# Three opening loads on another issuing queue, and a moved filter layer, in the prologue of a hybrid long-convolution and attention step

## The chip, the cores and the metric

The kernel runs on one core of a Trainium2 chip. The metric is the device time of one execution in microseconds (us). A program of one core is timed in several executions, and the median is given; one further execution is recorded by the hardware profiler.

## The reference, cut to what matters here

```python
shift, scale, gate = modulation(cond, w_ada, b_ada)        # silu(cond) @ w_ada + b_ada
h = x * (1 + scale) + shift                                # 128 context and 512 latent tokens, 1024 channels
hy, g_h, qkv, g_a, m = split(h @ w_in)                     # 10 x 1024 columns
z = concat([t, cos(bands * w), -sin(bands * w)])           # 33 features of each filter position
hf = sin(f_freq[0] * (z @ f_w1 + f_b1))                    # filter network, layer 1, 64 wide
hf = sin(f_freq[1] * (hf @ f_w2 + f_b2))                   # layer 2
y_h = long_conv(v_h, x1, x0, (hf @ f_w3) * decay)          # FFT convolution
y_a = attention(q, k, v)                                   # neighbourhood and context attention
out = (sigmoid(m) gates of (y_h*silu(g_h)) @ w_bh and (y_a*silu(g_a)) @ w_ba) @ w_out
x_new = layer_norm(ALPHA * x + gate * out)
```

All of it is in 32-bit floating point. The kernel gets this accuracy from TensorE's faster 32-bit form by cutting each operand into a high and a low part and adding three products (high by high, high by low, low by high).

## The kernel before, in words

All 640 tokens are held as columns; the 1024 channels lie in eight groups of 128 partitions. After an opening, the kernel works through 104 weight tiles of 128 output columns. A projection tile is 8 groups x 3 part products x 2 halves of 320 token columns: 48 products. The order on TensorE (PE), VectorE (DVE) and ScalarE (ACT) is written by hand in the opening; behind it a scheduler sets it, with a model of the time of each instruction. Every engine takes its own instructions in order.

**The opening** is `prologue` (from L267), a loop over the eight channel groups k. In each round

- SyncE (SP) issues two halves of modulation weights, `ada` (512 KB each, L258), and `xw` (L319, 512 KB: the group's tokens and three weight blocks). `xw` has three buffers (tag "raw", L307), which the later weight loads share; `ada` has three as well.
- PE multiplies the two halves by the conditioning vector (`adaT`, L262, 8 small products for each half). ACT copies the result (`row`, L318), PE turns it (`modT`, L341), DVE adds the biases (`mod`, L346).
- DVE and ACT make the modulated tokens: `hx` (L353) on DVE, the high part `hH` (L354) on ACT, the low part `hL` (L357) on DVE. `wf` (L328) and `wg` (L356) are the high and low parts of the three weight blocks.
- PE then makes the products of group k for tiles 0, 8 and 1 (`accumulate`, L172, its products stand at L177) in the next round; the table `script` (L268) says where. An entry "w3" in that table is three products of a zeroed operand (L281) whose result is thrown away; they fill PE's time.

Beside this runs **the filter network** (`hidden_layers`, L244). Each of its two layers (`sin_layer`, L222) is two products (L228), then a chain on DVE (L230 to L239) that reduces the angle, then ACT's sine (L241). The table `layers` (L272) says how many steps of it each round takes. Layer 1 works on `zemb` (33 x 640) and on `pack1` (128 x 196: both layers' weights, biases and frequencies); layer 2 on layer 1's `hf` and on `pack1`. The conditioning vectors and `sel` come in `pack0` (128 x 34). The buffer of `pack1` is used again for the first cached key block, `ck` (L865), so that load has to wait for the last reader of `pack1`, the two L230 of layer 2.

In the opening SP issues its loads in the order of the code: `pack0`, `zemb`, `pack1`, then round 0's `ada`. A load's completion is counted on one of eight counters in turn, and a load that would use a counter again waits for the load that used it before; so SP's order and the number of loads decide some of its waits.

**After the opening** come tiles 9 and 2, whose weights were loaded and split early, and then tile 10, the first whose low part is made by a transfer: ACT writes the negated high part to `wl` (L156) and GpSimd (POOL) issues a load of the weights that adds onto it (L157). Between them ACT and DVE evacuate the finished tiles 0, 8 and 1 (`zs`, L548 to L552), convolve them (`u` and `x`, L554 and L556), and split the transform's constants: `dftH` from `draw` (L381) and `gsH` from a block of `E` that the load `E<-gs` fills (L389, split at L391). The first filter products `fl` (L442, L443) need `w3h` and `w3l`, the split of the filter's last weights.

Of the kernel before, what the change touches and what calls it, by code (L numbers as in the profile page):

```python
# [46 lines left out]
def tile_hyena_natten_step(ctx: ExitStack, tc: tile.TileContext, a, o):  # L47
    nc = tc.nc
    P = 128

    def f(ap):
        return ap.bitcast(F32)
# [7 lines left out]
    pinned = [True]  # L60
    last = []

    def load_to(dst, src):
        ins = nc.sync.dma_start(dst, src)
        last[:] = [ins]
        if pinned[0]:
            tc.keep_in_program_order(ins)
# [33 lines left out]
    def aux(name):  # L101
        return ps_ax.tile([P, 512], F32, tag="aux", name=name)
# [9 lines left out]
    def row(pool, tag, name, dt=F32, bufs=NK + 1):  # L112
        return pool.tile([P, NT], dt, tag=tag, bufs=bufs, name=name)

    out = {"yh": {}}
    dram = ctx.enter_context(tc.tile_pool(name="dram", bufs=1, space=bass.MemoryType.DRAM))
    yh_d, ya_d, mh_d, ma_d = (dram.tile([NK, P, NT], F32, tag=t, name=t) for t in ("yh_d", "ya_d", "mh_d", "ma_d"))

    def load_pack(i):
        pack = const.tile([P, sum(n for _, n in PACKS[i])], F32, tag=f"pack{i}", name=f"pack{i}")  # L120
        load_to(pack[:], a[f"pack{i}"])
        c0 = 0
        for name, n in PACKS[i]:
            out[name] = pack[:, c0 : c0 + n]
            c0 += n

    v_d = dram.tile([4, P, 1280], F32, tag="v_d", name="v_d")

    load_pack(0)
    cc, sel = out["cc"], out["sel"]  # L130
    bss = const.tile([P, 2, NK], F32, tag="bss", name="bss")

# [7 lines left out]
    def wraw(i):  # L140
        raws[i] = wp.tile([P, 1024], F32, tag="raw", bufs=3, name=f"raw{i}")
        load_to(raws[i][:], a["wall"][i])
# [26 lines left out]
    def bank(i, ps_pair=None):  # L169
        return ps_pair or [acc(f"mm{i}_{hf}") for hf in range(2)]  # L170

    def accumulate(ps, w, k, xh, xl, lead=(0, 1, 2)):  # L172
        passes = (w[0], xh), (w[0], xl), (w[1], xh)
        for i in lead:
            wt, x = passes[i]
            for hf in range(2):
                nc.tensor.matmul(  # L177
                    ps[hf][:, :HALF], wt[k], x[:, hf * HALF : (hf + 1) * HALF],
                    start=(i == 0 and k == 0), stop=(i == lead[2] and k == NK - 1), skip_group_check=True,
                )  # L180
# [31 lines left out]
    def temp(tag, name, bufs=1):  # L212
        return hw.tile([P, NT], F32, tag=tag, bufs=bufs, name=name)
# [43 lines left out]
    def ada(ch, ps, raw):  # L257
        load_to(raw, a["wada"][ch])  # L258
        for t in range(2):
            for j in range(4):  # L260
                kt = 4 * t + j
                nc.tensor.matmul(  # L262
                    ps[32 * j : 32 * j + 32, :], st[:, kt, :], raw[:, P * kt : P * kt + P],
                    start=(t == 0), stop=(t == 1), skip_group_check=True, tile_position=(0, 32 * j),
                )

    def prologue():  # L267
        script = (  # L268
            ("w3", "w1", "w3", "w4"), ("", "", "00", "80 10"), ("", "", "01", "81 11"), ("", "", "02", "82 12"),
            ("", "", "03", "83 13"), ("", "", "04", "84 14"), ("", "", "05", "85 15"), ("", "", "06", "86 16 07 87 17"),  # L270
        )
        layers = ((1, 1), (0, 2), (0, 2), (0, 2), (1, 1), (0, 0), (0, 0), (0, 0))  # L272
        nc.vector.memset(f(hid[:, :256]), 0.0)
        front = (0, 8, 1)
        parts = {}

        def work(items):
            for item in items.split():
                if item[0] == "w":
                    for _ in range(int(item[1:])):  # L280
                        nc.tensor.matmul(banks[0][0][:, :256], hid[:, :P], hid[:, :256], start=True, stop=True, skip_group_check=True)  # L281
                else:
                    i, j = int(item[0]), int(item[1])
                    c = P * front.index(i)
                    accumulate(banks[i], [{j: t[:, c : c + P]} for t in parts[j]], j, hH[:, j], hL[:, j], lead=(0, 2, 1))

        def step(n):
            for _ in range(n):
                next(filt, None)

        out["zemb"] = temp("u", "zemb", 4)[:33]
        load_to(out["zemb"], a["zemb"])
        load_pack(1)
        th0 = const.tile([P, 2 * NK], F32, tag="th0", name="th0")
        spare = const.tile([P, 1], F32, tag="spare", name="spare")
        nc.gpsimd.memset(spare[:], 0.0)
        nc.scalar.activation(th0[:], cc, AF.Tanh, scale=0.5)
        nc.scalar.activation(spare[:], spare[:], AF.Sin)
        nc.vector.scalar_tensor_tensor(th0[:], th0[:], 1.0, cc, op0=ALU.add, op1=ALU.mult)
        nc.vector.tensor_scalar_mul(st[:, :, 0:2], th0[:].rearrange("p (k c) -> p k c", c=2), 0.5)  # L300
        nc.vector.tensor_copy(bss[:, 0], out["bss"][:, :NK])
        nc.vector.tensor_scalar_add(bss[:, 1], out["bss"][:, NK:], 1.0)
        for i in front:
            banks[i] = bank(i, (aux("mm1lo"), aux("mm1hi")) if i == 1 else None)
        filt = hidden_layers()
        for k in range(NK):
            xw = wp.tile([P, 1024], F32, tag="raw", bufs=3, name=f"xw{k}")  # L307
            psa = aux(f"adaT{k}")
            if k == 0:
                work("w12")  # L310
                step(7)
            pool, tag = ((hw, "X"), (hyc, "dftL"), (hw, "F"))[k % 3]
            wt = pool.tile([P, 2048], F32, tag=tag, name=f"ada{k}")
            for part in range(2):
                work(script[k][part])
                ada(part * 8 + k, psa[:, part * P : part * P + P], wt[:, 1024 * part : 1024 * part + 1024])
            row_ = hwa.tile([P, 2 * P], F32, tag="fb", bufs=3, name=f"row{k}")
            nc.scalar.activation(row_[:], psa[:, : 2 * P], AF.Copy)  # L318
            load_to(xw[:], a["xw"][k])  # L319
            xt, wf = xw[:, :NT], xw[:, NT:]  # L320
            wh = row(yhp, "yh", f"wf{k}", F32R)[:, : 3 * P]
            wl = row(yhp, "yh", f"wg{k}", F32R)[:, : 3 * P]
            parts[k] = wh, wl
            step(layers[k][0])
            if k >= 6:
                split(wh, wl, wf)
            else:
                nc.scalar.activation(wh, wf, AF.Copy)  # L328
            if k == 7:
                wraw(9)  # L330
                load_pack(2)
                out["convw"] = out["convw"].rearrange("p (i c) -> p i c", c=4)
                wraw(2)
                load_filter(0)
                out["dft"] = hw.tile([P, 2560], F32, tag="F", name="draw")
                load_to(out["dft"][:, :1280], a["dft"][:, :1280])
                w9 = hw.tile([P, 2, 1024], F32R, tag="X", name="w9")
            psm = aux(f"modT{k}")
            work(script[k][2])
            for c in range(2):  # L340
                nc.tensor.matmul(  # L341
                    psm[:, c * 2 : c * 2 + 2], row_[:, c * P : c * P + P], sel,
                    start=True, stop=True, skip_group_check=True,
                )
            mod = const.tile([P, 2, 2], F32, tag="mod", bufs=4, name=f"mod{k}")
            nc.vector.tensor_tensor(  # L346
                mod[:], psm[:, 0:4].rearrange("p (s c) -> p s c", s=2),
                bss[:, :, k : k + 1].to_broadcast([P, 2, 2]), op=ALU.add,
            )
            hx = hwa.tile([P, NT], F32, tag="cv", bufs=2, name=f"hx{k}")  # L350
            for c, s0, n in ((0, PC, LP), (1, SC, LS)):
                cs = slice(s0, s0 + n)
                nc.vector.tensor_scalar(hx[:, cs], xt[:, cs], mod[:, 1, c : c + 1], mod[:, 0, c : c + 1], op0=ALU.mult, op1=ALU.add)  # L353
                nc.scalar.activation(hH[:, k, cs], xt[:, cs], AF.Identity, scale=mod[:, 1, c : c + 1], bias=mod[:, 0, c : c + 1])  # L354
            if k < 6:
                nc.vector.tensor_tensor(wl, wf, f(wh), op=ALU.subtract)  # L356
            nc.vector.tensor_tensor(hL[:, k], hx[:], f(hH[:, k]), op=ALU.subtract)  # L357
            if k == 7:
                raw = raws.pop(9)
                nc.scalar.activation(w9[:, 0], raw[:], AF.Copy)  # L360
                low = nc.vector.tensor_tensor(w9[:, 1], raw[:], f(w9[:, 0]), op=ALU.subtract)
                early[2] = wtile(2)
                early[9] = [[w9[:, i, c : c + P] for c in range(0, 1024, P)] for i in range(2)]
            work(script[k][3])
            step(layers[k][1])
        now(filt)
        last.append(low)
# [1343 lines left out]
```

## Time and the profile before

| | us |
|---|---|
| three timed executions | 861.53, 862.32, 863.46 |
| their median | 862.32 |
| the profiled execution, its own time | 860.83 |
| its span, first to last instruction | 859.1 |
| PE busy in the span | 849.4 (99%) |
| DVE busy | 678.7 (79%) |
| ACT busy | 464.7 (54%) |

The span is 1.73 us shorter than the same execution's own time; what lies around the span is not in the profile. A PE that is shown as busy is not PE at its peak, since matmul ends are modelled; but where products follow one another at an even spacing, nothing but fewer or earlier products shortens the stretch. The page's mean transfer rate is 161 GB/s, and its first two slices of 21 us show 352 and 359.

### The profile page before, as it was taken

To read this page: it belongs to the slowest core of one execution; us is meant where nothing else is said; L and a number is where in the kernel's file an instruction comes from. 1 tells how busy PE (TensorE), PEld (TensorE's weight loads), DVE (VectorE), ACT (ScalarE), POOL (GpSimd) and SP (SyncE) were. 2 spreads that over 40 slices of the span, in tenths; PEclk is the share of its full clock that TensorE was granted. 3 is DMA by queue.
4 is the path that set the end of the run, shared out by engine and by line. 5 is a ranking of instruction groups with operands and counts; after the bars stand their busy time and mean duration, and the time that the engine had idled before them with its cause. 6 is when DMAs were issued, how large, how long until landed. Compare 5 with 4: busy or idle time off the path is not lost.

```text
span 859.1 us, 16817 instructions
## 1 busy us (share of the span) xinstructions
PE 849.4 (99%) x6387; PEld 822.7 (96%) x6387; DVE 678.7 (79%) x1408; ACT 464.7 (54%) x996; POOL 131.4 (15%) x140
## 2 busy tenths in 40 slices
PE   9999999999999999999999999999999999999996
PEld 7999999999999999999999999999999999999885
DVE  6777695697759559789988897889888778799776
ACT  4675656545554643646665676666655654345310
POOL 0010010101001010105232225124222200000000
PEclk9999999999999999999999999999999999999999
DMA  9986575656657558774263535354354386445621
GB/s 352 359 256 144 109 149 126 153 122 144 127 134 150 126 146 187 168 251 148 85 195 90 192 95 189 106 177 149 105 173 118 111 266 202 173 131 140 246 107 54
DMA packets 56868, 138.64 MB, mean 161 GB/s; under 512 B 8495, under 2 KB 23859, under 8 KB 56788
## 3 DMA queue, kind: packets, MB, share of 16 engines
q1 hardware_dynamic: 45412, 111.69, 39.7%
q0 software_dynamic: 5760, 20.19, 14.4%
q10 hardware_dynamic: 5616, 5.70, 1.9%
q8 instruction: 50, 0.82, 0.4%
q14 instruction: 30, 0.25, 0.1%
HBM read 121.43 MB, written 16.12 MB: 160 GB/s over the span
## 4 chain that ended last, share of the span: by engine, by line
PE 95%; DMA 3%; DVE 1%; SPq 0%; ACT 0%; issue 0%; DVEq 0%
PE sp L1182 33%; PE mm L177 30%; PE out L1534 6%; PE v L917 5%; PE pt L1019 3%; PE s L1026 3%; PE s L979 2%; PE mm L191 2%; PE ve L929 1%; DMA raw<-wall 1%; DMA wl<-wall 1%; DMA ada<-wada 1%; PE adaT L262 1%; PE yb L166 1%; PE yb L165 1%; PE yb L167 1%
## 5 line engine op out<-in xcount | busy, mean ns | idle before, releaser
L1182 PE MATMUL sp<-t,wb 128*128 128x320 f32 x912 | 141.7, 310 | 0.0
L1182 PEld LDWEIGHTS sp<-t,wb 128*128 128x128 f32 x912 | 134.9, 188 | 0.9 <-ACT pp L1047 0.5
L1182 PE MATMUL sp<-hH,wb 128*128 128x320 f32 x456 | 111.2, 314 | 0.0
L177 PE MATMUL mm<-hH,wl 128*128 128x320 f32 x448 | 105.5, 309 | 0.1
L177 PE MATMUL mm<-hH,wh 128*128 128x320 f32 x448 | 104.9, 309 | 0.0
L177 PE MATMUL mm<-hL,wh 128*128 128x320 f32 x448 | 104.2, 310 | 0.0
L157 POOL DMA_DIRECT2D wl<-wall x37 | 32.2, 870 | 329.5 <-ACT wl L156 263.3
L108 ACT ACTIVATE wb<-s 128x512 fp32r<-128x512 f32 x92 | 56.3, 627 | 45.6 <-DVE s L1142 26.6
L1182 PEld LDWEIGHTS sp<-hH,wb 128*128 128x128 f32 x456 | 78.4, 188 | 2.3 <-issue 2.1
L158 ACT ACTIVATE wh<-raw 128x1024 fp32r<-128x1024 f32 x37 | 39.2, 1059 | 70.8 <-PE mm L177 65.3
L177 PEld LDWEIGHTS mm<-hH,wl 128*128 128x128 f32 x448 | 75.5, 188 | 0.9 <-DMA wl<-wall 0.4
L177 PEld LDWEIGHTS mm<-hH,wh 128*128 128x128 f32 x448 | 75.2, 188 | 0.5
L177 PEld LDWEIGHTS mm<-hL,wh 128*128 128x128 f32 x448 | 75.1, 188 | 0.3
L109 DVE TENSOR_TENSOR wb<-s,wb 128x512 fp32r<-128x512 f32 x92 | 62.5, 692 | 10.3 <-ACT wb L108 10.3
L1182 PE MATMUL sp<-hL,wb 128*128 128x320 f32 x228 | 70.4, 309 | 0.0
L108 ACT ACTIVATE wb<-raw 128x512 fp32r<-128x512 f32 x66 | 41.4, 628 | 44.4 <-PE sp L1182 23.5
L1001 POOL TENSOR_SCALAR p<-p,sm 128x384 f32<-128x384 f32 x32 | 44.5, 1399 | 102.7 <-DVE sm L1000 102.7
L109 DVE TENSOR_TENSOR wb<-raw,wb 128x512 fp32r<-128x512 f32 x66 | 46.6, 705 | 5.5 <-ACT wb L108 5.4
L177 PE MATMUL mm<-yhs,wh 128*128 128x320 f32 x256 | 47.9, 309 | 0.0
L1197 DVE TENSOR_TENSOR c<-sp,u 128x320 f32<-128x320 f32 x69 | 33.5, 486 | 12.0 <-PE sp L1182 12.0
L1182 PEld LDWEIGHTS sp<-hL,wb 128*128 128x128 f32 x228 | 42.8, 188 | 0.0
L1001 POOL TENSOR_SCALAR edge<-edge,sm 128x320 f32<-128x320 f32 x32 | 41.9, 1318 | 0.5 <-DVE sm L1000 0.5
(385 smaller groups left out, 2078.3 us busy)
## 6 DMA issues: line engine op xcount, KB each, us to landing
raw<-wall SPq DMA_DIRECT2D x93, 512.0 KB, 3.6
wl<-wall POOLq DMA_DIRECT2D x37, 512.0 KB, 5.8
ada<-wada SPq DMA_DIRECT2D x16, 512.0 KB, 9.2
tm<-bias SPq DMA_DIRECT2D x16, 512.0 KB, 4.5
xw<-xw SPq DMA_DIRECT2D x8, 512.0 KB, 9.4
gate<-wgate SPq DMA_DIRECT2D x8, 512.0 KB, 4.1
wo<-wall SPq DMA_DIRECT2D x8, 512.0 KB, 5.3
dec<-decay SPq DMA_DIRECT2D x20, 128.0 KB, 3.0
```

The costliest lines, as they stand in the source:

```text
L108: hi = nc.scalar.activation(dst_h, src, AF.Copy)
L109: return hi, (eng or nc.vector).tensor_tensor(dst_l, src, f(dst_h), op=ALU.subtract)
L157: nc.gpsimd.dma_start(wl, a["wall"][i], accum_op=ALU.add)
L158: nc.scalar.activation(wh, raw[:], AF.Copy)
L177: nc.tensor.matmul(ps[hf][:, :HALF], wt[k], x[:, hf * HALF : (hf + 1) * HALF], start=(i == 0 and k == 0), stop=(i == lead[2] and k == NK - ...
L917: nc.tensor.matmul(ps[t // 2][:, t % 2 * 256 : t % 2 * 256 + 256], x[:, k, P * t : P * t + P], wk, start=first and t % 2 == 0, stop=last, ...
L1001: nc.gpsimd.tensor_scalar_mul(pv, pv, sm[:, 2:3])
L1019: nc.tensor.transpose(pt[:, i * P : i * P + P], x, ident)
L1026: nc.tensor.matmul(dst, lhs, rhs, start=start, stop=stop, skip_group_check=True)
L1182: nc.tensor.matmul(dst, wk, x(xi, k), start=j < 4 and k == 0 and i == 0, stop=k == 3 and i == 2, skip_group_check=True,)
L1197: after = nc.vector.tensor_tensor(c, dst, c if j == 3 else u, op=ALU.add)
L1534: ins = nc.tensor.matmul(dst, m[k][:, c0 : c0 + P], w[:, c : c + n], start=(first and k == 0), stop=(last and k == 5), skip_group_check=True,)
```

## The change

Three things change, all in the opening.

1. `pack0`, `zemb` and `pack1` are issued by ACT instead of SP, so SP's first load is round 0's `ada`.
2. The two products of the filter network's layer 2 move from behind round 0 to the middle of round 1: between the products of the two `ada` halves.
3. The filler products of round 0 go from 12, 3, 1, 3, 4 to 12, 2, 1, 3, 2.

```diff
-    def load_to(dst, src):
-        ins = nc.sync.dma_start(dst, src)
+    def load_to(dst, src, eng=nc.sync):
+        ins = eng.dma_start(dst, src)
...
-    def load_pack(i):
+    def load_pack(i, eng=nc.sync):
...
-        load_to(pack[:], a[f"pack{i}"])
+        load_to(pack[:], a[f"pack{i}"], eng)
...
-    load_pack(0)
+    load_pack(0, nc.scalar)
...
-            ("w3", "w1", "w3", "w4"), ("", "", "00", "80 10"), ("", "", "01", "81 11"), ("", "", "02", "82 12"),
+            ("w2", "w1", "w3", "w2"), ("", "", "00", "80 10"), ("", "", "01", "81 11"), ("", "", "02", "82 12"),
...
-        layers = ((1, 1), (0, 2), (0, 2), (0, 2), (1, 1), (0, 0), (0, 0), (0, 0))
+        layers = ((1, 0), (0, 2), (0, 2), (0, 2), (1, 1), (0, 0), (0, 0), (0, 0))
...
-        load_to(out["zemb"], a["zemb"])
-        load_pack(1)
+        load_to(out["zemb"], a["zemb"], nc.scalar)
+        load_pack(1, nc.scalar)
...
             for part in range(2):
                 work(script[k][part])
+                if k == 1 and part == 1:
+                    step(1)
                 ada(part * 8 + k, psa[:, part * P : part * P + P], wt[:, 1024 * part : 1024 * part + 1024])
```

Lines behind the insertion stand two lower in the changed kernel (L548 becomes L550). What the change moves on the engines, where it matters below:

On PE, from the transposed modulation of round 0 on (`modT0`; `ps_f640` are the products of layer 2, `adaT1` those of round 1's `ada` halves), the rows before were

```order
L341 MATMUL modT0_195<-pack0_84,row0_188 128x2 x2
L281 MATMUL mm0_0_134<-hid_93 128x256 x4
L228 MATMUL ps_f6400_214<-hf1_154,pack1_123 128x320
L228 MATMUL ps_f6401_215<-hf1_154,pack1_123 128x320
L262 MATMUL adaT1_221<-ada1_222,st_89 32x128 x16
L177 MATMUL mm0_0_134<-hH_87,wf0_191 128x320
```

and they are now

```order
L343 MATMUL modT0_194<-pack0_84,row0_187 128x2 x2
L281 MATMUL mm0_0_134<-hid_93 128x256 x2
L262 MATMUL adaT1_212<-ada1_213,st_89 32x128 x8
L228 MATMUL ps_f6400_223<-hf1_154,pack1_123 128x320
L228 MATMUL ps_f6401_224<-hf1_154,pack1_123 128x320
L262 MATMUL adaT1_212<-ada1_213,st_89 32x128 x8
L177 MATMUL mm0_0_134<-hH_87,wf0_190 128x320
```

The layer's two products stand eight small products later, and two fillers are gone here (one more stood behind layer 1). DVE's order in the opening is the same as before.

On ACT, behind the opening, the scheduler has set another order. Before, from the end of the evacuation of tile 0 on (`zs0`; `zs1` is tile 8, `u0` its first convolution):

```order
L552 ACTIVATE zs0_106<-mm0_1_135 128x8x40
L548 ACTIVATE zs1_110<-mm8_0_136 128x128
L550 ACTIVATE zs1_110<-mm8_0_136 128x8x8
L551 ACTIVATE zs1_110<-mm8_0_136 128x8x16
L552 ACTIVATE zs1_110<-mm8_1_137 128x8x40
L554 ACTIVATE u0_667<-zs0_106,pack2_601 128x641
L108 ACTIVATE w3h_0_694<-w3s0_696 128x512
```

and now

```order
L554 ACTIVATE zs0_106<-mm0_1_135 128x8x40
L108 ACTIVATE gsH_104<-E_100 128x256
L550 ACTIVATE zs1_110<-mm8_0_136 128x128
L552 ACTIVATE zs1_110<-mm8_0_136 128x8x8
L553 ACTIVATE zs1_110<-mm8_0_136 128x8x16
L554 ACTIVATE zs1_110<-mm8_1_137 128x8x40
L556 ACTIVATE u0_664<-zs0_106,pack2_598 128x641
L383 ACTIVATE dftH_102<-draw_608 128x640 x2
L108 ACTIVATE w3h_0_691<-w3s0_693 128x512
```

`gsH`, which stood behind `dftH` eleven rows further on, has moved ahead of the evacuation of tile 8; `dftH` has moved ahead of `w3h`. Behind these rows come, in both, the evacuation of tile 1 and the convolution `x`; then before `u1`, `wl10`, `wh10`, `wl3`, and now `wl10`, `wh10`, `u1`, `wl3` (`wl10` and `wh10` are tile 10's weights). On PE the first filter product moves 11 products later, and on DVE `gsL` and `dftL` come earlier. Behind tile 10 the orders are the same.

On SP the three small loads are gone from the front, and one load changes place. Before:

```order
L64 DMA ada3_340<-wada 128x1024 x2
L64 DMA xw3_338<-xw 128x1024
L64 DMA ada4_399<-wada 128x1024 x2
L64 DMA ck0_4395<-ck 128x128
L64 DMA xw4_397<-xw 128x1024
```

and now:

```order
L64 DMA ada3_337<-wada 128x1024 x2
L64 DMA xw3_335<-xw 128x1024
L64 DMA ck0_4392<-ck 128x128
L64 DMA ada4_396<-wada 128x1024 x2
L64 DMA xw4_394<-xw 128x1024
```

The load of `ck` stands ahead of round 4's `ada` now, so those wait on SP until `pack1`'s last reader is done.

## Prediction

> **What bounds the kernel now.** I read the page first, then busy time by stretch, then the chain that ended last at its beginning, then the engines' timelines there.
>
> ```profile
> PE 849.4 (99%) x6387; PEld 822.7 (96%) x6387; DVE 678.7 (79%) x1408; ACT 464.7 (54%) x996; POOL 131.4 (15%) x140
> ```
> ```profile
> 0.00:12.00 12.00, 10.14 (x101) 7.14 (x102) 6.70 (x19) 5.59 (x10) 0.87 (x16) 1.00 0.81 303
> 12.00:42.00 30.00, 30.00 (x355) 27.41 (x354) 21.44 (x44) 17.02 (x32) 0.00 (x0) 1.00 0.97 376
> 42.00:62.00 20.00, 19.91 (x135) 19.48 (x134) 15.87 (x24) 16.50 (x38) 2.74 (x3) 1.00 0.88 271
> 62.00:100.00 38.00, 38.00 (x270) 37.75 (x269) 25.57 (x45) 22.15 (x45) 3.45 (x4) 1.00 0.62 136
> ```
> ```profile
> 3.92 7.09 DMA ada<-wada
> 11.05 0.65 PE adaT L262 x16
> 11.69 1.07 PE mm L177 x6
> ...
> 49.73 1.07 ACT wl L156
> 51.11 7.61 DMA wl<-wall
> 58.77 1.15 PE mm L177 x6
> ```
>
> The first number behind a stretch is its length, the next PE's busy time. From 12 us on PE is full; only a fragment is missing at 42 to 62, where the chain shows PE waiting for the transfer that finishes tile 10's low weights. So the end moves by as much as PE's dense stretch starts earlier or later near 12 us, plus what PE loses around 58. The chain names what started it: the second half of round 1's `ada`, landed at 11.01. It is only the last of several things, as the timelines of PE, DVE and ACT (each asked alone) show:
>
> ```profile
> 1.17 2.93 PE L281 MATMUL mm<-hid 128*128 128x256 f32 x12 [1.17 <-DVE hid L273]
> 4.03 1.18 PE L228 MATMUL ps_f<-zemb,pack 33*64 33x320 f32 x4
> 11.62 0.56 PE L177 MATMUL mm<-hH,wf 128*128 128x320 f32 x2
> 12.31 0.46 PE L177 MATMUL mm<-hL,wf 128*128 128x320 f32 x2
> ```
> ```profile
> 5.26 0.61 DVE L230 TENSOR_SCALAR E<-ps_f,pack 128x320 f32<-128x320 f32 x1 [1.86 <-PE ps_f L228]
> 8.21 0.33 DVE L239 TENSOR_SCALAR E<-E 128x320 f32<-128x320 f32 x1
> 9.06 0.16 DVE L346 TENSOR_TENSOR mod<-modT,bss 128x4 f32<-128x4 f32 x1 [0.53 <-PE modT L341]
> 10.57 0.83 DVE L357 TENSOR_TENSOR hL<-hx,hH 128x640 fp32r<-128x640 f32 x1
> 11.32 1.12 DVE L230 TENSOR_SCALAR E<-ps_f,pack 128x320 f32<-128x320 f32 x2
> 13.14 0.16 DVE L346 TENSOR_TENSOR mod<-modT,bss 128x4 f32<-128x4 f32 x1 [0.70 <-PE modT L341]
> ```
> ```profile
> 8.57 0.47 ACT L241 ACTIVATE hf<-E 128x320 f32<-128x320 f32 x1 [0.20 <-DVE E L239]
> 9.36 1.19 ACT L354 ACTIVATE hH<-xw,mod 128x128 fp32r<-128x128 f32 x2
> ```
>
> There is a second chain, without slack inside. Layer 1's products (L228 at 4.03) feed DVE's angle chain, which ends at 8.54; ACT's sine follows at 8.57, and behind it in ACT's order `wf` and `hH` (9.36 to 10.55); then DVE's `hL` (to 11.40); then PE's first product with `hL` (12.31). From L228 to the end of `hL` it takes 11.40 - 4.03 = 7.37 us, and the chain loses its place as the second only by 12.31 - 11.40 = 0.9 us. **Whatever moves L228 moves the start of the dense stretch.**
>
> **The change, part by part.** The loads first, from SP's timeline and the transfer views:
>
> ```profile
> 0.73 0.38 SPq L64 DMA_DIRECT2D pack<-pack  x1
> 1.16 0.42 SPq L64 DMA_DIRECT2D zemb<-zemb  x1
> 1.63 0.35 SPq L64 DMA_DIRECT2D pack<-pack  x1
> 2.02 0.90 SPq L64 DMA_DIRECT2D ada<-wada  x2
> ```
> ```profile
> pack<-pack SPq DMA_DIRECT2D x1, 98.0 KB, 2.0
> ```
> ```profile
> DMA packets 737, 2.69 MB, mean 414 GB/s; under 512 B 80, under 2 KB 80, under 8 KB 737
> ...
> q1 hardware_dynamic: 737, 2.69, 101.9%
> ```
> ```profile
> q0 software_dynamic: 58, 0.24, 61.5%
> q1 hardware_dynamic: 70, 0.29, 41.0%
> ```
>
> (The last two are the queues from 4.5 to 11 us and from 54.5 to 56.5.) SP's first `ada` goes from 2.02 to 0.73, so its stream starts 1.29 us earlier and the half that landed at 11.01 comes near 9.7. By itself this frees PE's first dense product, and the second chain takes over: with L228 at 4.03, the first product with `hL` could go at about 4.03 + 7.42 = 11.45 (0.05 for the handover), a gain of 0.86.
>
> But the small loads lose their empty transfer engines. Before, `pack1` was issued at 1.63 and landed 2.0 later, at 3.63, while L228 waited for the fillers to end at 4.1. Now three small loads of ACT's queue run beside SP's stream of 4 KB packets. No row of before shows this pair of queues in the opening; the nearest is 54.5 to 56.5, where two queues that were both full sent 58 and 70 packets: about one for one, whatever their packets cost. From 4.5 to 11 a 4 KB packet takes 1.019 x 16 x 6.5 us / 657 = 0.16 us of an engine (737 packets less the 80 tiny ones). A load of 128 rows is 8 packets for each of 16 engines; `pack0` and `pack1` make 16, `zemb` (33 rows) two or three more. One for one, `pack1` lands 16 x 0.16 = 2.6 us later, at **6.2**; with `zemb` counted, at 6.7. The other bound is sharing by bytes: 0.2 MB of SP's beside the 0.2 MB of small loads at 414 GB/s, 0.5 us, landing at 4.1. The row I have says one for one, so I take 6.2. L228 then starts at 6.2, `hL` is ready at 13.6, and its first product moves from 12.31 to 6.2 + 7.42 = 13.62: **+1.3 us** (bounds -0.8 at 4.1 and +1.8 at 6.7; nothing is gained or lost at 4.9). PE takes its instructions in order, so the fillers, both `adaT`, `modT` and layer 2 queue behind L228 and cannot use the earlier `ada`; DVE's `mod` queues behind the angle chain.
>
> The Trainium skill ("DMA: Bandwidth & Descriptors", sections "Queues, rings and completion order" and "Issuing engines are not separate DMA queues") says that each transfer engine goes round its queues packet by packet, with some 9 to 17 descriptors to a packet, and that issuing from several engines saves only issue time, which speaks against this change. With whole loads of 8 rows taking turns, two loads of `ada` would stand ahead of `pack1`'s last, again 16 x 0.16 us, and the sum would be the same; 58 to 70 agrees with the turns and cannot tell their size.
>
> ACT's own cost: three issues of 0.4 us stand ahead of its table load, so `th` runs near 3.5 rather than 2.54, or behind a late `pack0`; the consumers of its result (`adaT`) wait for L228 anyway. Zero; with L228 at 4.1 the cover is the 5.2 us until L228 ends.
>
> Layer 2 between the halves: its products need `hf`, and `hH` is 1.5 us behind `hf`, so eight small products on either side cost nothing. Its L230 pair (1.12 us) follows `hL` as before and leaves `mod` of round 1 its 0.70 us of slack. The three fillers fall into waits: zero; gone cover would cost 3 x 0.2 us. `ck` ahead of round 4's `ada` holds SP until that L230 pair is done, about 14.7 instead of 11.75; PE needs that `ada` at 23.6 (the chain's row below), or 24.9 with the delay, while four loads of 512 KB, 5 us of transfer, are still queued: zero.
>
> ```profile
> 23.59 1.01 PE adaT L262 x32
> ...
> 61.38 4.11 PE mm L177 x28
> ```
>
> **The new order on ACT** behind the opening, from ACT's and SP's timelines and the transfers of 37.8 to 38.2:
>
> ```profile
> 42.86 0.29 ACT L548 ACTIVATE zs<-mm 128x128 f32<-128x128 f32 x1
> 46.48 1.44 ACT L381 ACTIVATE dftH<-draw 128x640 fp32r<-128x640 f32 x2
> 47.74 0.49 ACT L108 ACTIVATE gsH<-E 128x256 fp32r<-128x256 f32 x1
> 48.04 1.00 ACT L554 ACTIVATE u<-zs,pack 128x641 f32<-128x641 f32 x1
> 49.73 1.06 ACT L156 ACTIVATE wl<-raw 128x1024 fp32r<-128x1024 f32 x1 [0.69 <-DMA raw<-wall]
> ```
> ```profile
> 37.92 0.37 SPq L64 DMA_DIRECT2D draw<-dft  x1
> 38.33 0.44 SPq L64 DMA_DIRECT2D E<-gs  x1
> ```
> ```profile
> draw<-dft SPq DMA_DIRECT2D x1, 640.0 KB, 7.0
> ```
>
> `gsH` now stands where 42.86 is. Its load `E<-gs` follows `draw` on the same queue, and `draw` landed at 37.92 + 7.0 = 44.92; so I expect `E` at 44.9 to 45.3 and ACT held for 2.1 to 2.4 us (all times of this part move together with the start). Queued behind it are the evacuation of tile 8, `w3h`, and `wl10`. From there the work to `wl10` is `gsH` 0.30 (47.74 to 48.04) and the rows that filled 42.86 to 47.74, 4.88 us; `u1` has moved behind. `wl10` starts at 44.92 + 0.30 + 4.88 = 50.1, up to 50.5, against 49.73. PE waits for exactly this chain at 58.77, so it is **+0.4 to +0.75; I take 0.5**. The other waiters have slack: tile 2, which takes tile 8's banks, begins at 50.9 (`wh` in the row below), 5 us after the late evacuation, and the first filter product is 11 products of 0.147 us (4.11 / 28) later.
>
> ```profile
> 50.89 0.45 PE L177 MATMUL mm<-hH,wh 128*128 128x320 f32 x2
> ```
>
> If `E` landed by 42.9, this term would be zero.
>
> Sum: 1.3 + 0.5 = **+1.8 us**, in the profile's own terms from a span of 859.1 to 860.9 and from its own time of 860.83 to 862.6. That execution was 1.5 below the median of 862.32, so I add the change to the median: **864.1**.
>
> **The rivals.** (a) *The queues share by bytes, or the small packets slip through.* `pack1` lands by 4.1 to 4.6, L228 is hardly later, `ada` is early, and the gain of 0.86 to 0.3 meets the 0.5 of `gsH`: -0.4 to +0.2, **862.1**, not slower. It decides below a landing of 4.9. For it speaks that the small loads hold only 0.2 MB; against it the 58 to 70. (b) *It does all it says*: as (a), and `E` lands in time: -0.86, **861.5**. Against it, `draw`'s 7.0. (c) *PE falls back to its slow pace.* The 12 fillers start 0.24 us apart for 256 columns, where later products of 320 columns start 0.147 apart: PE begins at about half speed. If a gap of 2 us before L228 undoes the warming, the dense stretch could begin slow; 2.9 us of it, as long as the first fillers took, at half pace would be 1.5 us more, +3.3, **865.6**. Against it: the fillers and `adaT` run between. The profile's granted clock stands at 1.00 in the first stretch already and cannot show it. The Trainium skill ("TensorE: Matmul & The Clock Gate", "Part 1: The HAM clock gate (the "warmup" mystery)") puts the fall back to half pace after an idle window of about 3.4 us, and by that rule a gap of 2 us is too short. (d) *Nothing in it reaches the end*: excluded for the start, since PE has no idle time behind 12 us to absorb it.
>
> **How the numbers follow.** The forecast, small loads late and ACT held, 0.55, with its own range +1.2 to +2.6; (a) 0.25; (b) 0.08; (c) 0.07; mixtures 0.05. A measurement of this kernel can tell about 0.2%, 1.72 us, from no change. Half of the forecast's range lies above that, so slower 0.37 (0.28 of it, (c), and 0.02), same 0.60 (the other half, (a), (b) and some), faster 0.03. The range takes in the forecast's and (a)'s: 861.6 to 865.0.
>
> **What would show it.** L228 at 6 rather than 4 us, with PE idle before it and the wait put down to a load; `ada` no longer on the chain. If L228 starts by 4.6, the main step is wrong. In ACT's timeline a wait of about 2 us before `gsH`, and PE missing near 1 us before tile 10's low product, where 0.09 is missing now (19.91 of 20); if neither is there, the second step is wrong. Any loss behind 62 us would contradict the whole.

## The result and the profile after

| | before | after |
|---|---|---|
| median, us | 862.0 (861.25 to 863.56, 6 executions) | 870.2 (865.94 to 871.52, 6 executions) |
| profiled execution, its own time, us | 860.83 | 870.91 |
| its span, us | 859.1 | 869.1 |

The changed kernel takes 1.0083 times as long, with a 95% interval of 1.0056 to 1.0109: it is slower, by 8.2 us between the medians and by 7.2 by the ratio, where +1.8 was forecast, and outside the range of 861.6 to 865.0. The span grew by 10.0 us in the profiled pair.

The chain that ended last names the places. Its columns are start, length, what:

```profile
1.82 7.15 DMA pack<-pack
9.10 1.33 PE ps_f L228 x4
...
11.16 1.01 PE adaT L262 x16
...
19.31 1.51 PE mm L177 x6
...
31.62 1.01 PE adaT L262 x32
...
60.06 7.60 DMA wl<-wall
67.71 1.44 PE mm L177 x8
```

The chain no longer begins with the half of `ada` but with `pack1`: issued by ACT at 1.82, landed at 8.97. From then on PE itself is the chain. The `adaT` of round 4 stands at 31.62, where before had it at 23.59: **8.03 us are lost in the opening**, and all rounds behind it come at the old spacing. PE's timeline of the opening:

```profile
1.17 2.93 PE L281 MATMUL mm<-hid 128*128 128x256 f32 x12 [1.17 <-DVE hid L273]
9.10 1.33 PE L228 MATMUL ps_f<-zemb,pack 33*64 33x320 f32 x4 [5.00 <-DMA pack<-pack]
11.09 1.08 PE L262 MATMUL adaT<-ada,st 128*32 128x128 f32 x16
12.62 1.08 PE L262 MATMUL adaT<-ada,st 128*32 128x128 f32 x16
15.85 1.08 PE L262 MATMUL adaT<-ada,st 128*32 128x128 f32 x16
16.86 1.44 PE L228 MATMUL ps_f<-hf,pack 64*128 64x320 f32 x4
18.23 1.08 PE L262 MATMUL adaT<-ada,st 128*32 128x128 f32 x16
19.24 0.90 PE L177 MATMUL mm<-hH,wf 128*128 128x320 f32 x2
```

Two things are to be seen. Layer 1 starts at 9.10 instead of 4.03. And the groups behind it take 1.6 times as long: sixteen products of `adaT` take 1.08 us where they took 0.65, two products of `hH` 0.90 where they took 0.56. PE works at its slow pace until about 20 us.

The waits of PE (columns: total us, times, longest) give the rest:

```profile
PE ps_f L228 <- DMA pack<-pack: 5.0, 1, 5.0
PE mm L281 <- DVE hid L273: 1.2, 1, 1.2
PE mm L177 <- DMA wl<-wall: 1.0, 1, 1.0
PE sp L1184 <- DMA wb<-wall: 0.9, 1, 0.9
```

The third is the wait before tile 10's low product. Its cause is in ACT's timeline:

```profile
53.44 0.42 ACT L108 ACTIVATE gsH<-E 128x256 fp32r<-128x256 f32 x1 [2.42 <-DMA E<-gs]
```

Before, PE was idle there for 0.09 of 20 us (42 to 62); now it is idle for 1.0 of 20 us (50 to 70): +0.9. The fourth wait lies near 800 us and was not there in the profile of before. Sum: 8.03 + 0.9 + 0.9 = 9.8 of the 10.0.

What kept `pack1` is read from the packets of the two queues: q1 is SP's, q10 ACT's. The views are of 1.5 to 3.6 us, of 4.6 to 5.1 and of 5.5 to 8.5; the columns are packets, megabytes and the share of 16 engines' time:

```profile
q1 hardware_dynamic: 110, 0.45, 61.1%
q10 hardware_dynamic: 78, 0.01, 3.2%
...
q1 hardware_dynamic: 44, 0.18, 97.9%
...
q1 hardware_dynamic: 313, 1.13, 93.0%
q10 hardware_dynamic: 144, 0.10, 10.4%
```

In the first stretch the 17 KB of `pack0` go beside SP's packets, from 3.0 to 3.6 us 54 of ACT's and 54 of SP's. In the second ACT's queue sends nothing at all, 2.8 us after `pack1` was issued. In the third it sends 144 packets and 0.10 MB, which is all of `pack1` (128 rows and 16 completions), while SP sends its third load and most of its fourth.

### The profile page after: what moved, and what is told of

Same layout as the page of the kernel before. It is cut to its first block, busy times and chain, and to the rows that moved or that the text cites. A ratio compares the mean times of both kernels' runs of the same rounds, so it can differ in the third digit from the quotient of the medians.

```text
span 869.1 us, 16810 instructions
## 1 busy us (share of the span) xinstructions
PE 853.4 (98%) x6384; PEld 825.2 (95%) x6384; DVE 678.5 (78%) x1408; ACT 464.9 (53%) x996; POOL 131.5 (15%) x140
## 4 chain that ended last, share of the span: by engine, by line
PE 93%; DMA 3%; issue 1%; ACT 1%; DVE 1%; SPq 0%; ACTq 0%; DVEq 0%; POOLq 0%
PE sp L1184 31%; PE mm L177 30%; PE out L1536 6%; PE v L919 5%; PE pt L1021 3%; PE s L1028 3%; PE s L981 2%; PE mm L191 2%; PE ve L931 1%; PE adaT L262 1%; DMA wl<-wall 1%; DMA pack<-pack 1%; DMA wb<-wall 1%; DMA dinv<-dft 1%; PE yb L165 1%
```

## The experiments

Beside each kernel stands the kernel before, on the same chip; its median there was 861.7 to 861.9, and some of its executions took 864 to 867. Ratios are to that.

**1. Only the loads (e1_loads).**

```diff
-    load_pack(0)
+    load_pack(0, nc.scalar)
...
-        load_to(out["zemb"], a["zemb"])
-        load_pack(1)
+        load_to(out["zemb"], a["zemb"], nc.scalar)
+        load_pack(1, nc.scalar)
```

> Only the three small loads go to ACT; layer 2 and the fillers 12, 3, 1, 3, 4 stay as before. Theory A (the late pack1 does nearly all): pack1 lands near 9 us as in the changed kernel, layer 1's first product starts at 9.0 to 9.2, PE is at its slow pace behind the gap (16 products of adaT take about 1.08 us, 0.65 before), the adaT of round 2 comes 8 us later than at 14.97, and the time is 7 to 9.5 us above before. Theory B (the moved layer and the missing fillers do a part of it): the loads alone cost the lateness of pack1, about 5 us, PE recovers its pace by 16 us, and the time is 4 to 6 us above before.

Measured: 868.38 us (865.53 to 870.47), ratio 1.0073 (1.0053 to 1.0094). `pack1` landed at 8.96, layer 1 began at 9.10, and the sixteen `adaT` took 1.08 us; the `adaT` of round 2 came at 22.98, in the changed kernel at 22.96, before at 14.90. Theory A: the loads alone give the whole shift of the start.

**2. Only the layer and the fillers (e2_layer).** The changed kernel with `nc.scalar` taken out at the three loads.

> Only the moved layer and the fewer fillers; the three loads stay on SP. In this kernel gsH stands behind dftH on ACT, as before. Theory A: the first product of layer 1 at 4.0 us, adaT at 0.65 us for 16, the adaT of round 2 within 0.2 us of 14.97, and the time within 0.8 us of before. Theory B: PE's pace drops or the dense stretch starts late, and the time is 2 to 4 us above before.

Measured: 863.35 us (860.77 to 866.74, 12 executions), ratio 1.0011 (0.9994 to 1.0029): no difference that can be told. The profiled execution (863.70) did not go as theory A had it, though. Layer 1 began at 4.08 and the first `adaT` took 0.64; then PE waited 1.4 us for the second half of `ada`, from 8.46 on the `adaT` took 1.08, and round 2 came at 18.19. Here the profile's column of the granted clock shows it. The columns are the stretch, its length, PE's busy time and products, PEld, DVE, ACT, POOL, then the granted clock, the share of the transfer engines and GB/s:

```profile
4.00:6.00 2.00, 1.41 (x7) 0.62 (x6) 0.94 (x2) 0.42 (x2) 0.00 (x0) 1.00 0.91 348
6.00:8.00 2.00, 0.96 (x17) 0.59 (x17) 1.84 (x5) 0.00 (x0) 0.00 (x0) 0.96 1.01 383
8.00:10.00 2.00, 1.53 (x18) 1.11 (x19) 0.29 (x1) 0.39 (x2) 0.00 (x0) 0.50 1.03 414
10.00:12.00 2.00, 2.00 (x17) 1.76 (x19) 0.80 (x3) 1.40 (x4) 0.00 (x0) 0.50 1.03 418
12.00:14.00 2.00, 2.00 (x20) 0.81 (x12) 1.42 (x3) 0.56 (x1) 0.00 (x0) 0.50 1.01 416
14.00:16.00 2.00, 2.00 (x26) 1.69 (x24) 1.13 (x2) 0.80 (x2) 0.00 (x0) 0.84 1.05 424
16.00:18.00 2.00, 2.00 (x17) 1.99 (x15) 1.53 (x5) 1.20 (x2) 0.00 (x0) 1.00 1.00 403
```

PE is busy for some 60% of the time from 4 to 8 us; then its clock is halved, and it stays so until 14.7 although PE is busy all the time from 10 on. The trace's record gives the times: full from 4.41, half from 7.83, full from 14.65. The stretches are 3.413 and 6.827 us, one and two times the same length. So the opening stands near an edge even with the loads on SP. This is why the two terms had to be separated by experiments that hold the pace.

**3. The pace held (e3_fill).** The changed kernel with a longer first run of fillers.

```diff
-                work("w12")
+                work("w50")
```

> The changed kernel with 50 fillers in place of the first 12, so that PE stays at work from 1.2 to about 9 us. Theory A1 (the gap of 5 us lets PE fall back to its slow pace, which costs about 3 of the 8 us): layer 1's products start near 9.1 as in the changed kernel but take about 1.2 instead of 1.33 us, 16 products of adaT take 0.65 us, hL's chain sets the start again (first product with hL near 9.1 + 8.3 = 17.4 at most), and the time is 2 to 3.5 us below the changed kernel's, 866.5 to 868.5. Theory A2 (the slow pace isn't from the gap, or costs nothing, since the filter's angle chain is what lasts): adaT stays at 1.08 or the start stays where it was, and the time is within 1 us of the changed kernel's 870.2.

Measured: 865.11 us (864.53 to 866.19), ratio 1.0035 (1.0016 to 1.0053). PE's timeline:

```profile
1.18 7.52 PE L281 MATMUL mm<-hid 128*128 128x256 f32 x50 [1.18 <-DVE hid L273]
9.06 0.76 PE L228 MATMUL ps_f<-zemb,pack 33*64 33x320 f32 x4 [0.37 <-DMA pack<-pack]
10.18 0.65 PE L262 MATMUL adaT<-ada,st 128*32 128x128 f32 x16
11.07 0.65 PE L262 MATMUL adaT<-ada,st 128*32 128x128 f32 x16
...
16.05 0.56 PE L177 MATMUL mm<-hL,wf 128*128 128x320 f32 x2
...
18.75 1.08 PE L262 MATMUL adaT<-ada,st 128*32 128x128 f32 x32
```

`pack1` is as late as in the changed kernel, but PE is at its full pace, and 38 more products that compute nothing make the kernel 5.1 us faster by the medians (4.1 by the two ratios to the kernel before). Theory A1, with a larger size than expected (2 to 3.5). Round 2 stands at 18.75, against 14.90 before and 22.96 in the changed kernel. So of the 8.06 us **the late load costs 3.85 at full pace, and the slow pace 4.21**. The spans of the two profiles differ by 5.8 us, and nearly all of it is these 4.21, the wait near 800 us (0.9), which is not there, and a wait at tile 10 of 0.5 instead of 1.0. The spread shrank too: 1.7 us from the lowest to the highest, where the changed kernel has 5.6.

**4. Another order on ACT (e4_order).** Same loads, but `pack1`, `zemb`, `pack0`.

> The changed kernel with ACT's three loads in the order pack1, zemb, pack0. Theory S (the third load of ACT is stuck behind the 512 KB loads that SP has issued by then, whatever its size): pack1 as the first lands at 4 to 5.5 us and layer 1 starts at 4.1 to 5.5, but pack0 (17 KB, third) sends its first packet only after 5 us and lands at 6 to 9, and th waits for it; adaT then cannot start before 7.5, and the time is 2 to 6 us above before. Theory T (every packet of ACT's takes its turn with SP's, so what counts is the bytes ahead of a load): pack1 lands at 5 to 6.5, pack0 0.5 us behind it, and the time is 1 to 4 us above before; pack0's first packet goes before 5 us.

Measured: 867.74 us (864.98 to 869.03), ratio 1.0061 (1.0041 to 1.0080). `pack1`, now first, landed near 5.1; layer 1 waited for `zemb` and began at 5.54. `pack0`, of only 17 KB, became the late one:

```profile
1.82 6.32 DMA pack<-pack
8.94 1.08 PE adaT L264 x16
```

It landed at 8.14, and `adaT` had to wait for `st`, the conditioning vector that is made from `pack0`. Its first packet went at 5.55. Theory S on the loads (the time came to the upper end of its range, since PE was at the slow pace until 23 us): the third place is late, not the 98 KB.

**5. SP held behind its second load (e8_hold).** DVE writes one column of `xw`'s buffer behind `st`, so SP's third load has to wait until 5.9; it would overwrite that column anyway.

```diff
             if k == 0:
+                nc.vector.memset(xw[:, :1], 0.0)
                 work("w12")
```

> The changed kernel, and SP's third load (xw of round 0), with all behind it, held until DVE has made st (about 5.5 us): SP has only the two halves of ada out when ACT issues pack1 at 1.8. Theory H (pack1 stands in one line behind SP's third load, which isn't taken before the first is done): pack1's first packet goes at 2.8 to 3.5, it lands at 4.3 to 5.3, and layer 1 starts at 4.4 to 5.4, 4 us before the changed kernel. Theory Q (ACT's queue takes a third load only when its first has landed): pack1's first packet goes 0.4 to 0.6 after pack0 has landed, near 5, and layer 1 starts at 5.8 to 6.6. Time 1 to 6 us above before by H, 3 to 8 by Q, by the pace of PE.

Measured: 865.39 us (862.84 to 869.34), ratio 1.0041 (1.0025 to 1.0056). `pack1`'s first packet went at 5.18, not at 2.8 to 3.5, and layer 1 began at 6.81. Theory H in that form falls: SP's third load was not out yet. Theory Q was not met either, since 5.18 is only 0.2 after `th`, the first step of `st`, began to use `pack0` (5.00). What does fit is that 5.18 is the moment when the first completion of SP's *second* load was written. In the changed kernel ACT's third load began at 5.57 and the 16 completions of SP's second were written from 5.16 to 5.84; in e4_order, where `pack0` is ACT's third, these are 5.55 and 5.37 to 5.98. Hence a new theory, L: the two queues take turns by whole loads.

**6. SP held behind its first load (e9_hold1).** The same, with a column of the second half of `ada`.

```diff
             if k == 0:
+                nc.vector.memset(wt[:, 1024:1025], 0.0)
                 work("w12")
```

> The changed kernel, and SP held behind its first load (one half of ada) until DVE has made st (about 5 us). Holding SP behind its second load moved pack1's first packet only from 5.6 to 5.2 us, and in both runs it went when the second half of ada finished (first completions at 5.16 and 5.18). Theory L (the loads of the two queues are taken in turns, whole load by whole load, so that ACT's third load starts when SP's second is done; none is out here): pack1's first packet goes behind zemb's, at 3.6 to 4.5, and it lands at 4.5 to 5.4; layer 1 starts at 4.6 to 5.5. Theory Q (ACT's queue starts a third load only when its first has landed, near 5): first packet at 4.6 to 5.6, landing at 5.8 or later, layer 1 at 5.9 or later. The second half of ada comes near 8, so the time is 1 to 5 us above before by either.

Measured: 865.93 us (864.97 to 866.93), ratio 1.0040 (1.0028 to 1.0053). The packets from 3.7 to 4.6 us:

```profile
q10 hardware_dynamic: 238, 0.19, 63.1%
q1 hardware_dynamic: 18, 0.01, 3.2%
```

ACT's queue has the engines to itself there. Layer 1 in PE's timeline:

```profile
5.24 1.33 PE L228 MATMUL ps_f<-zemb,pack 33*64 33x320 f32 x4 [1.14 <-DMA pack<-pack]
```

As soon as SP's one load is done, ACT's queue sends everything that it has, 0.19 MB in 0.9 us; `pack1`'s first packet goes at 3.77, and layer 1 begins at 5.24. `pack0` had landed only at 4.7, so Q falls. **Theory L: ACT's third load starts when SP's second is done, and with no second load there is no wait.** The time is 4 us above before all the same: the second half of `ada`, held back here, is now on the chain that ends last, and PE was at its slow pace until 15.7.

**7. `pack1` first on SP (e5_pack1).**

```diff
-        load_pack(1, nc.scalar)
+        load_pack(1)
```

> The changed kernel with pack1 back on SP, as its first load; pack0 and zemb stay on ACT, so ACT has no third load. Theory H (ACT's third load is held behind SP's third in one line): pack1 lands by 3 us; zemb, ACT's second, lands near 5 as in the changed kernel, so layer 1's first product starts at 4.9 to 5.4 and the start is late by 0.5 to 1.5 us where PE is at its full pace; with the slow pace, which a gap of 1 us may bring, 3 us more. Time 861.5 to 866, at least 4 us below the changed kernel's 870.2. Rival (any small load in the opening beside SP's stream lands late, whichever engine issues it): pack1 from SP lands after 5, and the time is that of the changed kernel.

Measured: 861.32 us (860.20 to 865.99, 12 executions), ratio 0.9995 (0.9977 to 1.0012): no difference from before that can be told, and 9 us below the changed kernel by the medians. The rival falls, since `pack1` landed 2.1 us after its issue. `zemb`, behind the smaller stream, let layer 1 begin at 4.35. In this kernel `gsH` stands behind `dftH` again, which is a part of the 9 us. The execution that was profiled is the longest of the twelve, 865.99:

```profile
4.35 1.33 PE L228 MATMUL ps_f<-zemb,pack 33*64 33x320 f32 x4 [0.25 <-DMA zemb<-zemb]
6.34 1.08 PE L262 MATMUL adaT<-ada,st 128*32 128x128 f32 x16
...
20.44 1.08 PE L262 MATMUL adaT<-ada,st 128*32 128x128 f32 x32
```

No load is late there, and the chain is still lost to the slow pace: round 2 stands at 20.44, 5.5 us later than before.

**8. Only `pack0` on ACT (e10_zp).** `zemb` and `pack1` are SP's first loads, the fillers are those of before.

> The changed kernel with zemb and pack1 as SP's first two loads, only pack0 on ACT, and the fillers of before (12, 3, 1, 3, 4). Theory: nothing small is issued behind a large load of the other queue; pack1 lands by 3.5 us, layer 1 starts at 4.0 to 4.2 behind the fillers, the first halves of ada come 0.4 us earlier, and the time is 0 to 0.6 us below before (860.8 to 862.3), with the same late executions at 863 to 866 where PE's pace isn't raised in time. Rival (pack0 on ACT lands late and st holds adaT): adaT starts after 6.1 and the time is 0.3 to 1 above before.

Measured: 863.28 us (861.46 to 864.62), ratio 1.0006 (0.9993 to 1.0019), no difference. `st` did not hold `adaT` much (6.23), so not the rival; but the expected gain was not there either. In the profiled execution (864.24) layer 1 begins at 4.03, exactly as before, and the first product with `hL` goes at 15.24 instead of 12.31. Full clock is first on record at 14.2, and PE's list has no wait in the opening but the first one, for DVE, which is in every profile; so these 2.9 us are put down to the slow pace.

**9. `gsH` back behind `dftH` (e6_fillgs).** On top of e3_fill, since its times are close together.

```diff
-        split(gsH[:], gsL[:], gs)
+        hi, _ = split(gsH[:], gsL[:], gs)
+        behind(hi, dftH_done[-1])
```

> The kernel of the 50 fillers (865.1 us), and gsH held behind dftH on ACT, where it stands before. Theory: ACT's wait of about 2 us before gsH goes, PE's wait for tile 10's low weights falls from 0.5 us to 0.25 or less, and the time is 0.2 to 0.6 us below that kernel's. Rival: that wait is set by the transfer of the low weights or by the loads' order, not by ACT; PE's wait stays at 0.5 and the time is the same within 0.2.

Measured: 864.67 us (864.03 to 865.34), ratio 1.0030 (1.0019 to 1.0040), against 865.11 for e3_fill, which ran on another occasion. What decides is the list of PE's waits. In e3_fill it was

```profile
PE mm L281 <- DVE hid L273: 1.2, 1, 1.2
PE mm L177 <- DMA wl<-wall: 0.5, 1, 0.5
PE ps_f L228 <- DMA pack<-pack: 0.4, 1, 0.4
```

and in this kernel it is

```profile
PE mm L281 <- DVE hid L273: 1.2, 1, 1.2
```

The wait for tile 10's low weights, 0.5 us, is gone with the order (and `pack1` was not waited for this time, since the fillers ran to 9.4). The theory holds; the rival falls.

**10. More fillers in the kernel before (e7_warm).** 12, 6, 6, 3, 4 in place of 12, 3, 1, 3, 4.

> The kernel before with the fillers 12, 6, 6, 3, 4 in place of 12, 3, 1, 3, 4; loads and layers as before. The times of the kernel before lie at 861 to 862 in most of its executions and at 864 to 867 in 6 of 19. Theory P (those late executions are ones in which PE fell back to its slow pace in the gaps of the opening): with the gaps filled they are gone; all times lie within 860.8 to 862.8, the median is 861.0 to 861.8. Rival (they come from the transfers, the first halves of ada landing late): the spread stays, with times above 864 in a quarter of the executions. In this kernel the scheduler puts gsH early on ACT, as in the changed kernel, which may cost 0.3 to 0.7.

Measured: 862.54 us (860.96 to 863.97, 12 executions), ratio 1.0000 (0.9989 to 1.0012). `gsH` stands on ACT as before here, not early as the expectation has it. None of the times is above 864, but the bulk lies at 862 to 863.4, so neither theory was met. In the profiled execution (863.05) PE rises to its full pace only at 9.6; until then the added fillers run at the slow pace and cost time themselves. That they cut the worst cases is not shown: of the 35 executions of before beside it 6 took more than 864, of these 12 none, which can be chance.

**11. Fewer fillers in the kernel before (e11_cold).** 4 in place of the first 12; the loads stay on SP.

```diff
-                work("w12")
+                work("w4")
```

> The kernel before with 4 instead of 12 fillers ahead of layer 1; the loads on SP. Theory C (the slow pace alone costs 3 to 4 us, without any late load): layer 1 starts earlier, at 3.6 to 3.8 us, but PE stays at its slow pace, 16 products of adaT take 1.08 us, and the time is 2 to 4.5 us above before, 864 to 866.3. Rival (the pace costs nothing by itself, the late pack1 does): the start is 0 to 0.4 us earlier and the time within 0.7 of before. In this kernel the scheduler puts gsH early on ACT, which may cost up to 0.7 in either case.

Measured: 863.85 us (860.89 to 866.31, 12 executions), ratio 1.0014 (0.9998 to 1.0030). Seven executions lie at 863.7 to 866.3, as theory C has it, five at 860.9 to 862.7, so the median is not told from before. The profiled one (865.73) shows the price: layer 1 begins earlier, at 3.72, and the first product with `hL` goes at 15.57, 3.3 us later than before. PE is at the slow pace until 16.4. It also has the wait near 800 us, 1.1 us, and `gsH` stands early on ACT here.

## Why the prediction was wrong, point by point

**What bounds the kernel: right.** The loss in the opening went through to the end one for one, and nothing more was lost behind tile 10 than the short wait near 800. That the end moves with the start, and that moving L228 moves the start, is what happened. The chain behind L228 was right in size too: from the measured 9.06 of e3_fill the prediction's 7.42 us give 16.48 for the first product with `hL`, and it went at 16.05. The wait near 800 (0.9 us) is a loss that the prediction had ruled out.

**The landing of `pack1`: the step that failed first.** The prediction let the queues alternate packet by packet from the first packet on and put the landing at 6.2, with 6.7 as the bound. Measured: 8.97. The first load of each queue did go nearly one for one (78 packets to 110, and 54 to 54 from 3.0 us on). But ACT's third load waited for SP's second to finish, and only then shared with SP's third and fourth. It is the loads that take turns: `pack1` had the third place, behind two loads of 512 KB. The working had looked at this case and found "the sum would be the same"; it had counted two loads of 1.3 us each, ahead of the *last* packet. In the trace the two halves took until 4.1 and 5.8 us, they stood ahead of the *first*, and `pack1` itself took from 5.6 to 8.3. With PE at its full pace that makes 3.85 us of the start (e3_fill) where 1.3 stood.

The Trainium skill ("DMA: Bandwidth & Descriptors", section "Queues, rings and completion order") says that an engine drains a packet of some 9 to 17 descriptors from one queue before it goes to the next. Eight rows and a completion are 9, so a wait for a whole load agrees with e8_hold and e9_hold1. That one queue is drained before the next has its turn does not agree: 78 of the 128 rows of `pack0` had gone by 3.6 us, when the first of the 16 completions of SP's first load was written. Why a load that is beside another shares row by row, and the next one waits for a whole load, is open.

**Rival (c), PE's slow pace: dismissed, and half of the loss.** It had a chance of 0.07 and 1.5 us. In the profiled execution it took 4.2 us (22.96 against 18.75 for round 2). The question was put wrongly: whether a gap of 2 us undoes the warming. PE had not been warmed. The twelve fillers ran at the slow pace to their end at 4.10 (their starts lie 0.21 us apart, not 0.24), and the trace's record shows full clock first at 4.92 in the profile of before, during layer 1, and at 20.2 in that of after. The profile's column stood at 1.00 in the first stretch of both, as it shows nothing until the first change on record; only the lengths of equal groups (0.65 or 1.08) tell the pace there. And "the fillers and `adaT` run between" did not count for much: from 9.1 to 20.2 PE was busy without a gap, and the clock did not rise.

The rule from the Trainium skill ("TensorE: Matmul & The Clock Gate", "Part 1: The HAM clock gate (the "warmup" mystery)") that stood there was the one on falling back, which was beside the point. The one that mattered stands in the same section of the Trainium skill: a free-running window of 3.413 us has to be busy before the clock rises. The stretches of 3.413 and 6.827 us in e2_layer's record agree with the window; that a busy one is enough does not agree, since from 9.99 to 16.81 us the changed kernel had two that were busy throughout, and no rise. That the fall needs an idle window doesn't agree: in e2_layer PE was busy for about 2 of the 3.4 us in which it lost the pace.

**The change's other parts.** The fillers and the moved layer: costed at zero, and e2_layer cannot tell them from zero (1.0011, 0.9994 to 1.0029). ACT's hold before `gsH`: 2.42 us where 2.1 to 2.4 were forecast. Its price at tile 10: +0.9 where 0.4 to 0.75 stood and 0.5 was taken; e6_fillgs shows that the order on ACT makes it. Its size follows ACT's hold. In the six profiles with `gsH` early PE's wait is 1.0 and 1.3 us where ACT was held for 2.42 and 2.47 (the changed kernel, e1_loads), 0.5 at 1.83 (e3_fill), 0.2 at 1.39 (e4_order), and none is listed at 1.38 and 1.40 (e8_hold, e11_cold). Why `E` came so much later in some is open. **The wait near 800 us** is in the profiles of after and of four experiments, 0.2 to 1.1 us, and not in the other seven nor in before. One of those four, e7_warm, has the loads and ACT's order of before, so neither is needed for it. Its cause was not tried.

**The other rivals.** (a) and (b), the loads slipping through: did not happen; but with `pack1` moved to SP's front the rest of the change comes out at 861.3, which cannot be told from (b)'s 861.5 nor from before. (d) falls with the 8 us.

## What to carry to other kernels

A small load that something waits for belongs ahead of the stream, on the queue that carries the stream (`pack1` landed 2.0 to 2.3 us after its issue there): on another queue it had to wait here for whole large loads, and its place in its own queue counted for more than its size. Where a kernel opens at TensorE's slow pace, ask of each delay not only how long PE waits, but whether the wait falls before the clock has risen; the fillers of e3_fill and e6_fillgs lasted past the rise, and in the other kernels the first run of fillers ended before it. To tell the two apart, hold one fixed: here 38 more idle products gave back 4.2 of the 8.1 us at the start.

## What the runs showed of the hardware

- Two issuing queues with loads of 128 rows: the first two loads of the one ran beside the first two of the other, and ACT's third started as SP's second completed (5.57, 5.55 and 5.18 us against first completions at 5.16, 5.37 and 5.18); with no second load on SP it went at once (3.77).
- PE's clock changed in units of 3.413 us: in all thirteen profiles the time from the last rise on record to the fall at the end is a whole number of them (246 to 251). The first full clock came between 4.1 and 5.8 us in four profiles (before, e2_layer, e3_fill, e6_fillgs) and between 9.6 and 23 us in the other nine, among them e10_zp and e11_cold, which have no late load.
- It matters where in such a unit the fillers begin. Counted back from the rise, the units that take in most of the first twelve fillers begin at 1.51 in before, 1.00 in e2_layer and 0.56 in e10_zp, and PE's work is the same there, the fillers from 1.17 to 4.10 and layer 1 from 4.03 or 4.08. PE is busy for 3.41, 3.23 and 2.80 us of the unit, and the clock rises at its end in the first two only; in e3_fill 2.92 us were enough. That this is why one kernel's executions differ by 4 to 6 us, and those of e3_fill and e6_fillgs by 1.3 to 1.7, is argued from these four, not shown.
- Being busy was not enough to raise the clock: in the changed kernel PE worked without a gap from 9.1 us, mostly on small products (`adaT`, `modT`, both layers), and the clock rose at 20.2. Two whole units (9.99 to 13.40 and 13.40 to 16.81) passed busy without a rise, and so did one in e7_warm (2.77 to 6.18), by the profile, whose ends of products are modelled. Which property of these products counts was not tried.
